# Matmul operands at equal SBUF places, and a gate stage without GpSimd's share, in a two-layer hybrid trunk

## The chip, the cores and the metric

The kernel runs on one core of a Trainium2 chip. The metric is the device time of one execution in microseconds; lower is better. The program is one long, fully unrolled list of instructions for five engines: TensorE (PE in the profile; PEld are its weight loads), VectorE (DVE), ScalarE (ACT), GpSimd (POOL) and SyncE (SP), which here only issues DMAs.

## The reference, cut to what matters

Two layers act on 1024 positions of 1024 features. Layer 0 mixes positions with multi-head latent attention, layer 1 with gated linear attention (GLA). Each is followed by a gated convolutional FFN, and every residual sum goes through a LayerNorm. At the end of each layer an embedding is added through a gate:

```python
for i in range(DEPTH):                     # DEPTH = 2
    m = mla_mixer(x, ...) if i % 2 == 0 else gla_mixer(x, ...)
    x = layer_norm(DN_ALPHA * x + m, ln1_g[i], ln1_b[i])
    x = layer_norm(DN_ALPHA * x + conv_ffn(x, ...), ln2_g[i], ln2_b[i])
    gate = jax.nn.sigmoid(x @ ple_w_gate[i] + ple_b_gate[i])
    x = x + gate * (p[i] @ ple_w_proj[i])
```

The last two lines are the gate stage of this text.

## The kernel before, in words

**Split matmuls.** The results must have nearly float32 precision. Each operand is therefore kept as two float32r tiles, a high part `hi` and a residual `lo`; `mm3` (L178) makes a product of three matmuls: lo times hi, hi times lo, hi times hi. Weights are loaded as float32 by a DMA and split by `split`: ScalarE writes the high part, GpSimd or VectorE the low part (L139, L141).

**Layouts.** The residual stream is `acc`, eight tiles of 128 positions by 1024 features. Matmuls need it feature-major, so TensorE transposes blocks of it (with `ident`), and the result `xt` is two halves `f` of 512 positions, each with a high and a low tile of 8 blocks `k`.

**Order.** Instructions stand in the order in which a planner put them when the program was built, from dependences and its own cost model; each engine then works through its list in order. `tc.issue_after(ins)` keeps an instruction behind another one on its engine. Tiles come from pools; a buffer that is reused is waited for.

**Places.** A pool's tiles lie one behind the other in each partition of the SBUF. `pos_i`, eight int32 of 32 bytes, lies in the pool `mla`, and all pools opened behind it on the same side start 32 bytes further on. `pos_f` (32 bytes) and `blk` (120 bytes) shift what follows them in the same way. In the compiled program the places modulo 256 bytes are: query products `cq` 0 and `wq` 224; the first stage `win` 0 and `xT` 160; scores `kk`, `q`, `r` 0 and `ckv` 224; values `pT`, `vv` 0; output product `wo` and `o` 224; and down, up, gate and GLA products 224 for both operands.

**The gate stage.** The second LayerNorm of a layer is done by halves in `layer_norm_half`. `normalize` makes mean and deviation per tile and writes the normalised tile back to `acc`, without gain and bias. `turned` (L672, L666) transposes four blocks of 128 into a PSUM block of 512 and ScalarE writes it, with gain and bias, to `y`. VectorE copies `y` to the high part (L683), and GpSimd (every first block) or VectorE (every second) subtracts to get the low part (L684). Half 0 is done while the down projection of the FFN (`dn_ps`, additions at L1058) still runs on the tiles of half 1; half 1 is done in `ple`, under the first gate matmuls.

`ple` runs over two column halves `c` and eight tiles `t`: 24 matmuls for the gate (`g_ps`), 6 for the projected embedding (`pr_ps`). VectorE adds the gate's bias (L1142), ScalarE takes the sigmoid (L1143), VectorE multiplies with the projection (L1144) and adds the product to `acc` (L1145). As `acc` lacks gain and bias, `residual` applies them once per tile when `c` is 0: GpSimd multiplies with the gain's row (L815), VectorE adds the bias's row (L817), 1024 elements each. `turn_p` transposes the embeddings into `pT` (L1104 to L1106).

In layer 0 `feature_major` (L1117 to L1120) turns each finished tile for the GLA. It writes to new tiles `nx` in the buffers of `xt`, so it starts when the gate matmuls of half 0 are done: tiles 0 to 3 are turned behind the gate tiles 4 to 7, tiles 4 to 7 behind the last one. The GLA then starts with its gates (`a_ps` L1255, L1259).

Of the kernel before, what the change touches and what calls it, by code (L numbers as in the profile page):

```python
# [7 lines left out]
F32 = mybir.dt.float32  # L8
F32R = mybir.dt.float32r
BF16 = mybir.dt.bfloat16  # L10
I32 = mybir.dt.int32
AF = mybir.ActivationFunctionType
ALU = mybir.AluOpType
# [3 lines left out]
P = 128  # L17
S = 1024
D = 1024
NT = S // P  # L20
HALF = 512
# [21 lines left out]
def hybrid_trunk_kernel(ctx: ExitStack, tc: tile.TileContext, a: dict, out: bass.AP):  # L43
    nc = tc.nc
# [33 lines left out]
    neg_half = cpool.tile([P, 4], F32, name="neg_half")  # L78
    nc.vector.memset(neg_half, -0.5)
    half_pi = cpool.tile([P, 1], F32, name="half_pi")  # L80
    nc.vector.memset(half_pi, HALF_PI)

    par = {}
# [124 lines left out]
    with tc.tile_pool(name="pa", bufs=1) as pa, tc.tile_pool(name="pa2", bufs=2) as pa2:  # L208
# [21 lines left out]
                split(st, w_in[k][0][:, c0:c1], w_in[k][1][:, c0:c1], nc.vector if k % 2 else nc.gpsimd)  # L230


        pos_i = mla.tile([P, NT], I32, name="pos_i")
        nc.sync.dma_start(pos_i, a["positions"][0].rearrange("(t p) -> p t", p=P))
        pos_f = pa.tile([P, NT], F32, name="pos_f")
        nc.vector.tensor_copy(pos_f, pos_i)
        inv_b = pa.tile([P, 32], F32, name="inv_b")
        nc.sync.dma_start(inv_b, a["c_inv"].partition_broadcast(P))
# [383 lines left out]
            for f in range(2)  # L622
        ]

    ln_end = [None, None]
    fm_end = [None]

    xs = [dram.tile([P, D], F32, name=f"xs_{t}") for t in range(NT)]
# [26 lines left out]
    def turned(f, i, which, k, y, wide=True):  # L655

        g, b = par[f"ln{which}g", i], par[f"ln{which}b", i]
        if wide:
            y2 = big(f"y_ps_{i}_{which}_{f}_{k}")
            yps = [y2[:, :512], y2[:, 512:]]  # L660
        else:
            yps = [one(f"y_ps_{i}_{which}_{f}_{k + n}") for n in range(2)]
        for n in range(2):
            kn = k + n
            turn_block(f, kn, yps[n])
            nc.scalar.activation(  # L666
                y[:, n * HALF : (n + 1) * HALF], yps[n], AF.Identity, bias=b[:, kn : kn + 1], scale=g[:, kn : kn + 1]
            )

    def turn_block(f, k, dst):  # L670
        for tt in range(4):
# [2 lines left out]
    def layer_norm_half(f, i, which, tmp, xt, wide=True):  # L674

        normalize(f, i, which)
        for k in range(0, 8, 2):
            y = tmp.tile([P, S], F32, tag="tmp", name=f"y_{i}_{which}_{f}_{k}")
            turned(f, i, which, k, y, wide)
            for n in range(2):  # L680
                yn = y[:, n * HALF : (n + 1) * HALF]
                hi, lo = xt[f][0][:, k + n, :], xt[f][1][:, k + n, :]
                nc.vector.tensor_copy(hi, yn)  # L683
                ln_end[n] = (nc.vector if n else nc.gpsimd).tensor_tensor(lo, yn, hi, op=ALU.subtract).ins  # L684

    def first_half(i, tmp, xt, ys):

# [114 lines left out]
    def load_rows(pool, i, which):  # L802
# [4 lines left out]
            nc.sync.dma_start(t, a[f"ln{which}_{n}"][i].partition_broadcast(P))  # L807
            rows.append(t)
        return rows

    def residual(ts, rows, after=None):

        for t in ts:
            with tc.issue_after(ln_end[0]):
                nc.gpsimd.tensor_tensor(acc[t], acc[t], rows[0], op=ALU.mult)  # L815
            with tc.issue_after(after or ln_end[1]):
                nc.vector.tensor_tensor(acc[t], acc[t], rows[1], op=ALU.add)  # L817

    def up_stage(i, xt, tmp, sp, xb):

# [265 lines left out]
    def ple(i, xt, tmp, apool, sgp, gb, last):  # L1086
# [22 lines left out]
            turn_p(f)  # L1109
        bg = gb.tile([P, D], F32, tag="rowp", name=f"row_p_{i}")  # L1110
        nc.sync.dma_start(bg, a["ple_b_gate"][i].partition_broadcast(P))
        nx = []

        def feature_major(t):
            yp = big(f"x3_ps_{i}_{t}").rearrange("p (k n) -> p k n", k=8)
            for k in range(8):
                nc.tensor.transpose(yp[:, k, :], acc[t][:, k * P : (k + 1) * P], ident)  # L1117
            hi, lo = (n[:, :, (t % 4) * P : (t % 4 + 1) * P] for n in nx[t // 4])
            fm_end[0] = nc.scalar.copy(hi, yp).ins
            nc.vector.tensor_tensor(lo, yp, hi, op=ALU.subtract)  # L1120

        for c in range(2):
# [8 lines left out]
            for t in range(NT):  # L1131
                tl = slice((t % 4) * P, (t % 4 + 1) * P)
                gp = one(f"g_ps_{i}_{c}_{t}")
                for k in range(8):
                    mm3(gp, both(xt[t // 4], slice(None), k, tl), both(wgs[k // 2], slice(None), k % 2), k == 0, k == 7)
                rp = one(f"pr_ps_{i}_{c}_{t}")
                for k in range(2):
                    mm3(rp, both(pT[k], slice(None), slice(t * P, (t + 1) * P)), both(wpr, slice(None), k), k == 0, k == 1)
                if c == 0:
                    residual((t,), rows2[0])  # L1140
                sg = sgp.tile([P, HALF], F32, tag="sg", name=f"sg_{i}_{c}_{t}")
                nc.vector.tensor_tensor(sg, gp, bg[:, cs], op=ALU.add)  # L1142
                nc.scalar.activation(sg, sg, AF.Sigmoid)  # L1143
                nc.vector.tensor_tensor(sg, rp, sg, op=ALU.mult)  # L1144
                nc.vector.tensor_tensor(acc[t][:, cs], acc[t][:, cs], sg, op=ALU.add)  # L1145
                if last:
                    nc.sync.dma_start(out[0, t * P : (t + 1) * P, cs], acc[t][:, cs])
                elif c and t >= 4:
                    if not nx:
                        nx.extend(new_xt(f"x3_{i}"))  # L1150
                    feature_major(t - 4)
        if not last:
            for t in range(4, NT):
                feature_major(t)
        return nx

    def open_up(i, xt, tmp):

# [51 lines left out]
    with ExitStack() as pg:  # L1210
# [17 lines left out]
        def gates(g0):  # L1228
# [11 lines left out]
            tri = g0.tile([P, P], F32R, name="tri")  # L1240
            nc.vector.tensor_copy(tri, st[:, :P])

            blk = g0.tile([P, 30], F32R, name="blk")
            nc.vector.tensor_copy(blk, st[:, P : P + 30])
            w2 = g0.tile([2 * RANK + 1, 512], F32, name="w2")
            for r in range(2):
# [276 lines left out]
```

## Time and profile before

| | us |
|---|---|
| median of 3 runs | 3052.33 (3052.01 to 3053.41) |
| the profiled execution | 3054.3 |
| its span, first to last instruction | 3052.5 |
| PE busy | 2922.6 (96%) |
| DVE busy | 1725.6 (57%) |
| POOL busy | 1339.9 (44%) |
| ACT busy | 1251.5 (41%) |

The busy times are those of one profiled execution. Matmuls overlap in the pipeline, so their busy time is longer than their pace; the pace is read from starts or from the length of unbroken pieces. The mean granted clock of TensorE is 0.984 of 2.4 GHz; the profile knows two levels, 2.4 and 1.2 GHz.

### The profile page before, as it was taken

How to read it: one execution, taken by the hardware profiler on the slowest of the kernel's cores; microseconds unless marked ns; L12 is line 12 of the kernel's file. 1: busy time of each engine (PE TensorE's matmuls, PEld its weight loads, DVE VectorE, ACT ScalarE, POOL GpSimd, SP SyncE). 2: the span in 40 equal slices, each digit the busy share in tenths (PEclk: the TensorE clock that was granted, in tenths of full speed). 3: DMA queues.
4: the chain of work that ended last, by engine and by line, in shares of the span. 5: the costliest groups of instructions: out<-in, count | busy, mean ns of one | idle time of the engine just before them, and what ended most of it. 6: DMA issues, size and time to landing. Idle time of an engine off the chain costs nothing.

```text
span 3052.5 us, 36344 instructions
## 1 busy us (share of the span) xinstructions
PE 2922.6 (96%) x13938; PEld 2407.8 (79%) x13938; DVE 1725.6 (57%) x2815; ACT 1251.5 (41%) x2022; POOL 1339.9 (44%) x904
## 2 busy tenths in 40 slices
PE   8999999999988999999998999999979999999979
PEld 7878888888866888878877678888758888778867
DVE  5546666666675555545577444544765555545693
ACT  3325555555555444441131243333554544512231
POOL 4331101010056777765744113223358777666560
PEclk9999999999999999999999999999989999999999
DMA  3464212121123222253311102112122222343211
GB/s 117 134 236 155 70 54 67 56 68 52 37 83 97 83 83 82 78 171 97 124 49 37 48 23 63 30 47 62 62 83 85 82 83 76 118 138 118 90 49 49
DMA packets 197784, 254.66 MB, mean 83 GB/s; under 512 B 11297, under 2 KB 133961, under 8 KB 195562
## 3 DMA queue, kind: packets, MB, share of 16 engines
q1 hardware_dynamic: 193354, 230.32, 23.8%
q10 hardware_dynamic: 4256, 22.02, 2.0%
q8 instruction: 109, 1.79, 0.2%
q14 instruction: 65, 0.53, 0.1%
HBM read 191.49 MB, written 60.82 MB: 83 GB/s over the span
## 4 chain that ended last, share of the span: by engine, by line
PE 76%; DVE 7%; ACT 5%; POOL 4%; issue 4%; DMA 1%; SPq 0%; POOLq 0%; ACTq 0%; DVEq 0%
PE up_u L178 13%; PE dn_ps L178 13%; PE up_g L178 11%; PE g_ps L178 4%; PE m_ps L178 4%; PE gkv_ps L178 4%; PE o_ps L178 3%; PE gr_ps L178 3%; PE q_ps L178 3%; PE gm_ps L178 2%; PE pT_ps L542 2%; PE qr_ps L178 1%; PE k_ps L178 1%; PE v_ps L178 1%; ACT pr L526 1%
## 5 line engine op out<-in xcount | busy, mean ns | idle before, releaser
L178 PE MATMUL up_u<-xT_hi,wT 128*128 128x512 f32 x1056 | 346.4, 394 | 20.6 <-ACT acc L914 15.5
L1058 DVE TENSOR_TENSOR acc<-dn_ps,acc 128x512 f32<-128x512 f32 x320 | 220.0, 689 | 168.1 <-PE dn_ps L178 167.4
L178 PE MATMUL dn_ps<-wdn_hi,a_lo 128*128 128x512 f32 x704 | 277.0, 393 | 9.9 <-ACT acc L1054 6.4
L178 PE MATMUL dn_ps<-wdn_hi,a_hi 128*128 128x512 f32 x704 | 275.8, 392 | 0.0
L178 PE MATMUL dn_ps<-wdn_lo,a_hi 128*128 128x512 f32 x704 | 275.6, 391 | 0.0
L178 PEld LDWEIGHTS up_u<-xT_hi,wT 128*128 128x128 f32 x1056 | 200.2, 190 | 71.4 <-issue 19.2
L178 PE MATMUL up_g<-x_hi,wB 128*128 128x512 f32 x704 | 235.1, 394 | 5.2 <-DVE mv L639 1.6
L141 POOL TENSOR_TENSOR wo_lo<-wo_st,wo_hi 128x1024 fp32r<-128x1024 f32 x16 | 38.5, 2407 | 453.9 <-ACT wo_hi L139 453.9
L141 POOL TENSOR_TENSOR wT<-ws_S,wT 128x512 fp32r<-128x512 f32 x128 | 165.7, 1295 | 120.1 <-ACT wT L139 119.4
L178 PE MATMUL up_u<-xT_lo,wT 128*128 128x512 f32 x528 | 207.8, 394 | 0.0
L178 PE MATMUL m_ps<-wo_hi,o 128*128 128x512 f32 x512 | 190.8, 415 | 0.0
L141 POOL TENSOR_TENSOR wdn_lo<-wdn_st,wdn_hi 128x1024 fp32r<-128x1024 f32 x44 | 106.0, 2415 | 166.5 <-ACT wdn_hi L139 145.1
L139 ACT CAST wdn_hi<-wdn_st 128x1024 fp32r<-128x1024 f32 x44 | 45.7, 1048 | 304.9 <-PE dn_ps L178 287.2
L178 PEld LDWEIGHTS dn_ps<-wdn_hi,a_lo 128*128 128x128 f32 x704 | 133.0, 189 | 40.6 <-ACT acc L1054 8.1
L178 PEld LDWEIGHTS up_g<-x_hi,wB 128*128 128x128 f32 x704 | 132.0, 188 | 40.7 <-ACT acc L911 7.0
L178 PEld LDWEIGHTS dn_ps<-wdn_hi,a_hi 128*128 128x128 f32 x704 | 132.8, 189 | 27.8
L178 PEld LDWEIGHTS dn_ps<-wdn_lo,a_hi 128*128 128x128 f32 x704 | 133.1, 189 | 26.8
L141 POOL TENSOR_TENSOR wB<-wup_g,wB 128x512 fp32r<-128x512 f32 x84 | 111.3, 1329 | 85.4 <-ACT wB L139 85.3
L923 DVE TENSOR_TENSOR up_g<-up_g,acc 128x512 f32<-128x512 f32 x44 | 30.8, 700 | 208.2 <-PE up_g L178 201.3
L544 ACT CAST pT<-pT_ps 128x512 fp32r<-128x512 f32 x192 | 89.3, 475 | 139.2 <-PE pT_ps L542 136.9
L178 PE MATMUL o_ps<-pT,vv 128*128 128x512 f32 (+3 forms) x576 | 142.5, 350 | 3.8 <-ACT pT L544 2.9
L178 PE MATMUL up_g<-x_lo,wB 128*128 128x512 f32 x352 | 137.4, 390 | 0.2 <-DVE x_lo L702 0.2
(363 smaller groups left out, 8155.9 us busy)
## 6 DMA issues: line engine op xcount, KB each, us to landing
a_s<-acc SPq DMA_DIRECT2D x44, 512.0 KB
a_st<-a_s SPq DMA_DIRECT2D x44, 512.0 KB
wdn_st<-in_ffn_w_down_dram SPq DMA_DIRECT2D x44, 512.0 KB
wup_g<-in_ffn_w_up_dram SPq DMA_DIRECT2D x42, 512.0 KB
wup_u<-in_ffn_w_up_dram SPq DMA_DIRECT2D x42, 512.0 KB
q<-q_s SPq DMA_DIRECT2D x32, 512.0 KB
q_s<-qo ACTq DMA_DIRECT2D x14, 1024.0 KB
r<-r_s SPq DMA_DIRECT2D x32, 256.0 KB
```

Source lines behind the costliest of these rows:

```text
L139: nc.scalar.copy(hi, src)
L141: lo_last[0] = (lo_eng or nc.gpsimd).tensor_tensor(lo, src, hi, op=ALU.subtract).ins
L178: nc.tensor.matmul(ps, w[a_], x[b_], start=start and n == 0, stop=stop and n == 2, skip_group_check=more)
L526: nc.scalar.activation(pr, pr, AF.Copy, scale=ri)
L542: nc.tensor.transpose(tp[:, i * P : (i + 1) * P], prs[i][:, kb * P : (kb + 1) * P], ident)
L544: nc.scalar.copy(pT[:, 0, off:], tp[:, off:])
L923: nc.vector.tensor_tensor(g1, g1, self.u2, op=ALU.add)
L1058: put[t, c] = nc.vector.tensor_tensor(y, dp, y, op=ALU.add).ins
```

## The change

- `pos_i` moves to the first pool, padded to 64 int32; `pos_f` is padded to 32 elements, `blk` to 64. Both operands of all matmuls of the products get equal places modulo 256 bytes.
- In `layer_norm_half` ScalarE writes the high part itself from the PSUM block, a second time with gain and bias, in place of VectorE's copy of `y`. All low parts are VectorE's.
- `residual` is gone. Per half tile, behind the product with the projection, VectorE multiplies the half of `acc` with the gain's row, adds the bias's row to the gated product, and adds the two.
- `feature_major` writes into `xt` itself, in the columns of a tile whose gate matmuls are done, and so follows every gate tile of `c` = 1 by one; only tile 7 is left behind the last.

```diff
+    pos_i = cpool.tile([P, 64], I32, name="pos_i")[:, :NT]
...
-        pos_i = mla.tile([P, NT], I32, name="pos_i")
         nc.sync.dma_start(pos_i, a["positions"][0].rearrange("(t p) -> p t", p=P))
-        pos_f = pa.tile([P, NT], F32, name="pos_f")
+        pos_f = pa.tile([P, 32], F32, name="pos_f")[:, :NT]
...
+        return yps
...
-            turned(f, i, which, k, y, wide)
+            yps = turned(f, i, which, k, y, wide)
             for n in range(2):
-                yn = y[:, n * HALF : (n + 1) * HALF]
-                hi, lo = xt[f][0][:, k + n, :], xt[f][1][:, k + n, :]
-                nc.vector.tensor_copy(hi, yn)
-                ln_end[n] = (nc.vector if n else nc.gpsimd).tensor_tensor(lo, yn, hi, op=ALU.subtract).ins
+                kn, yn = k + n, y[:, n * HALF : (n + 1) * HALF]
+                hi, lo = xt[f][0][:, kn, :], xt[f][1][:, kn, :]
+                nc.scalar.activation(
+                    hi, yps[n], AF.Identity, bias=par[f"ln{which}b", i][:, kn : kn + 1], scale=par[f"ln{which}g", i][:, kn : kn + 1]
+                )
+                nc.vector.tensor_tensor(lo, yn, hi, op=ALU.subtract)
...
-    def residual(ts, rows, after=None):
-
-        for t in ts:
-            with tc.issue_after(ln_end[0]):
-                nc.gpsimd.tensor_tensor(acc[t], acc[t], rows[0], op=ALU.mult)
-            with tc.issue_after(after or ln_end[1]):
-                nc.vector.tensor_tensor(acc[t], acc[t], rows[1], op=ALU.add)
...
-            hi, lo = (n[:, :, (t % 4) * P : (t % 4 + 1) * P] for n in nx[t // 4])
+            hi, lo = (n[:, :, (t % 4) * P : (t % 4 + 1) * P] for n in xt[t // 4])
...
-                if c == 0:
-                    residual((t,), rows2[0])
                 sg = sgp.tile([P, HALF], F32, tag="sg", name=f"sg_{i}_{c}_{t}")
                 nc.vector.tensor_tensor(sg, gp, bg[:, cs], op=ALU.add)
                 nc.scalar.activation(sg, sg, AF.Sigmoid)
-                nc.vector.tensor_tensor(sg, rp, sg, op=ALU.mult)
-                nc.vector.tensor_tensor(acc[t][:, cs], acc[t][:, cs], sg, op=ALU.add)
+                sgi = nc.vector.tensor_tensor(sg, rp, sg, op=ALU.mult).ins
+                y = acc[t][:, cs]
+                with tc.issue_after(sgi):
+
+                    nc.vector.tensor_tensor(y, y, rows2[0][0][:, cs], op=ALU.mult)
+                    nc.vector.tensor_tensor(sg, sg, rows2[0][1][:, cs], op=ALU.add)
+                    nc.vector.tensor_tensor(y, y, sg, op=ALU.add)
                 if last:
                     nc.sync.dma_start(out[0, t * P : (t + 1) * P, cs], acc[t][:, cs])
-                elif c and t >= 4:
-                    if not nx:
-                        nx.extend(new_xt(f"x3_{i}"))
-                    feature_major(t - 4)
+                elif c and t:
+                    feature_major(t - 1)
         if not last:
-            for t in range(4, NT):
-                feature_major(t)
-        return nx
+            feature_major(NT - 1)
+        return xt
...
-            blk = g0.tile([P, 30], F32R, name="blk")
+            blk = g0.tile([P, 64], F32R, name="blk")[:, :30]
```

## Rows read from the trace of the kernel before

**Rows 1.** The page: share of the chain that ended last, by engine.
```profile
PE 76%; DVE 7%; ACT 5%; POOL 4%; issue 4%; DMA 1%; SPq 0%; POOLq 0%; ACTq 0%; DVEq 0%
```

**Rows 2.** Windows: length, busy times of PE, PEld, DVE, ACT, POOL, clock, DMA share, GB/s.
```profile
1580.00:1640.00 60.00, 44.26 (x186) 34.28 (x184) 51.88 (x52) 17.70 (x22) 41.72 (x24) 0.86 0.13 36
2908.00:2966.00 58.00, 42.02 (x193) 32.67 (x194) 52.88 (x53) 18.31 (x23) 43.12 (x24) 0.94 0.13 41
1724.70:1781.50 56.80, 49.54 (x195) 30.76 (x193) 38.77 (x57) 29.70 (x42) 12.84 (x5) 0.88 0.26 75
```

**Rows 3.** The chain in order of time: start, length, engine, tile, line, count.
```profile
124.78 11.20 PE q_ps L178 x48
...
425.42 1.39 PE m_ps L178 x6
...
1358.19 193.47 PE dn_ps L178 x852
...
1654.14 5.44 PE g_ps L178 x24
```

**Rows 4.** Timeline of PE, first stage: start, length, instruction; 17 starts apart.
```profile
79.81 0.40 PE L178 MATMUL h_ps<-win_hi,xT_lo 128*128 128x512 f32 x1
...
83.78 0.40 PE L178 MATMUL h_ps<-win_hi,xT_hi 128*128 128x512 f32 x1
```

**Rows 5.** Timeline of PE in the GLA, behind transposes; eight starts apart each.
```profile
1871.76 0.40 PE L178 MATMUL gr_ps<-x_hi,gwr_hi 128*128 128x512 f32 x1
...
1873.62 0.39 PE L178 MATMUL gr_ps<-x_lo,gwr_hi 128*128 128x512 f32 x1
...
1875.43 0.39 PE L178 MATMUL gr_ps<-x_hi,gwr_lo 128*128 128x512 f32 x1
```

**Rows 6.** Groups of DVE from 1560 to 1646: busy us, mean ns, idle before.
```profile
L817 DVE TENSOR_TENSOR acc<-acc,row_b 128x1024 f32<-128x1024 f32 x8 | 18.8, 2353 | 0.0
L684 DVE TENSOR_TENSOR x_lo<-y,x_hi 128x512 fp32r<-128x512 f32 x8 | 14.6, 1831 | 0.1
```

**Rows 7.** Timeline of DVE and POOL from 1603 to 1646.
```profile
1603.03 0.41 DVE L683 CAST x_hi<-y 128x512 fp32r<-128x512 f32 x1
...
1609.03 23.34 POOL L815 TENSOR_TENSOR acc<-acc,row_g 128x1024 f32<-128x1024 f32 x8
...
1617.33 3.35 DVE L817 TENSOR_TENSOR acc<-acc,row_b 128x1024 f32<-128x1024 f32 x1
...
1640.12 1.21 DVE L817 TENSOR_TENSOR acc<-acc,row_b 128x1024 f32<-128x1024 f32 x1
```

**Rows 8.** Groups of ACT from 1560 to 1646.
```profile
L666 ACT ACTIVATE y<-y_ps,par 128x512 f32<-128x512 f32 x16 | 11.7, 776 | 5.8 <-PE y_ps L672 5.6
```

**Rows 9.** Waits from 1575 to 1650: total us, times, longest.
```profile
PE pT_ps L1104 <- DVE pT_lo L1106: 8.0, 1, 8.0
...
PE pr_ps L178 <- POOL wpr_lo L141: 2.9, 1, 2.9
...
PE dn_ps L178 <- DVE acc L1058: 1.6, 1, 1.6
```

**Rows 10.** Timeline of PE from the last gate matmul to the GLA's gates.
```profile
1724.69 1.91 PE L1117 MATMUL x_ps<-ident,acc 128*128 128x128 f32 x16
1730.35 3.33 PE L1117 MATMUL x_ps<-ident,acc 128*128 128x128 f32 x16 [3.75 <-DVE x_lo L1120]
...
1744.53 3.59 PE L1255 MATMUL a_ps<-x_hi,aw 128*32 128x512 f32 x8 [1.05 <-DVE ge L1267]
```

**Rows 11.** Groups of DVE from 1646 to 1724, GpSimd mostly idle.
```profile
L1145 DVE TENSOR_TENSOR acc<-acc,sg 128x512 f32<-128x512 f32 x12 | 8.3, 693 | 0.4
...
L1142 DVE TENSOR_TENSOR sg<-g_ps,row_p 128x512 f32<-128x512 f32 x12 | 8.3, 691 | 36.0 <-PE g_ps L178 36.0
```

**Rows 12.** Timeline from 1622: ACT writes half 1, PE reads half 0.
```profile
1622.50 0.59 ACT L1105 CAST pT_hi<-pT_ps 128x512 fp32r<-128x512 f32 x1 [11.95 <-PE pT_ps L1104]
...
1622.68 0.63 PE L178 MATMUL pr_ps<-wpr_hi,pT_hi 128*128 128x512 f32 x1
```

More of the change, by code (lines that the diff above doesn't have):

```diff
@@ L623, in new_xt @@
         ]
-    ln_end = [None, None]
     fm_end = [None]
@@ L1111, in ple @@
         nc.sync.dma_start(bg, a["ple_b_gate"][i].partition_broadcast(P))
-        nx = []
         def feature_major(t):
```

## The prediction

> **What bounds the kernel now.** I began with the page, at the chain that ended last: TensorE carries 76% of it, VectorE 7%, ScalarE 5%, GpSimd 4% [rows 1]. So time can come from two places: from the pace of single matmuls, and from the few stretches where TensorE waits. I looked for both.
>
> *Pace.* In the chain, long unbroken pieces of matmuls with 512 columns show it as length over count. The down projection runs 852 in 193.47 us, 227.1 ns each; the query projection runs 48 in 11.20 us, 233.3 ns each; in the attention six matmuls of the output projection take 1.39 us, 231.7 ns each [rows 3]. In the first stage 17 steps from one start to another take 3.97 us, 233.5 ns each [rows 4]. The granted clock is full there, so this is no clock. The places differ: the compiled program of the kernel before puts, modulo 256 bytes, weights and activations of the down projection both at 224, those of the query projection at 224 and 0, those of the first stage at 0 and 160. A stream at equal places is not always fast either: after transposes the GLA projection starts at 232.5 ns a step (8 steps in 1.86 us) and then settles at 226 (8 steps in 1.81 us) [rows 5]. I read this as a pace that has to lock: a long stream at equal places locks after some eight matmuls, a stream at unequal places never does.
>
> *Waits.* The windows show where TensorE loses most. In layer 0 it is busy 44.26 us of the 60 us around the start of the gate stage, at a mean clock of 0.86; in layer 1 42.02 of 58 at 0.94; in the passage from the gate stage to the GLA 49.54 of 56.8 at 0.88 [rows 2]. A mean of 0.86 over the two levels 2.4 and 1.2 GHz means 28% of the stretch at the lower, so the loss is 15.7 us of idling and about 16.8 x 0.74 / 2 = 6.2 us of slow work: 22 us. In the same way layer 1 loses 16.0 + 2.5 = 18.5 us, the passage 7.3 + 5.9 = 13 us.
>
> What TensorE waited for in layer 0 is VectorE above all: 8.0 us for the transposed embeddings' low part, 2.9 us for GpSimd's low part of the projection's weights, 1.6 us for the down projection's additions [rows 9]. VectorE is late because its own instructions are stretched. The residual's addition takes 3.35 us while GpSimd runs its eight multiplications, a block of 23.34 us, and 1.21 us once GpSimd has finished [rows 7]; the mean low part takes 1831 ns and the mean addition 2353 ns [rows 6], against 0.69 us for half the size beside an idle GpSimd [rows 11]. The two engines get in each other's way.
>
> **The change part by part.**
>
> *Places.* Query and rotary products: 384 + 192 = 576 matmuls, 233.3 - 227.1 = 6.2 ns each, 3.6 us. First stage: 192 matmuls of 512 columns, 6.4 ns each, 1.2 us, less the first eight of every run of 24: 0.8 us. Attention: 128 groups of six output matmuls lose 6 x (231.7 - 227.1) = 28 ns each, 3.5 us, and scores and values perhaps as much again. These streams are short and cut by transposes, and the output matmuls were at equal places already, so most of the loss should stay: I take 2.5 us between 0 and 7. The gates' few matmuls get nothing. Sum 7 us, bounds 0 (places do nothing) and 12 (all of it locks).
>
> The Trainium skill (TensorE: Matmul & The Clock Gate, Step-by-step: what each phase is for) speaks against it: matmul data and weights come through two independent read ports, and loading weights takes nothing from the running matmul. By that rule this part is 0; it is a rival below, since rows 3 and 4 show streams that differ in pace.
>
> *High parts on ScalarE.* Each of the 8 blocks of a half loses VectorE's copy and gains a second reading of the same PSUM block, 776 ns [rows 8]. Per half 8 x 0.78 = 6.2 us more on ScalarE. The second half of the norm lies under four gate tiles of the first half. One has 24 matmuls in 5.44 us [rows 3] and six more at the same pace, 6.8 us, so the cover is 27 us. ScalarE works 17.7 us in the 60 us of this window [rows 2]; even if all of it fell under the cover, 24 of 27 us would be full. The first half lies under the last matmuls of the down projection. Without cover the move would cost 6.2 us a half, 25 us in all. The low parts all go to VectorE: four more per half, at about 0.69 us, against eight copies of some 0.41 us saved [rows 7]: nothing on balance.
>
> *GpSimd out of the stage.* Its 8 low parts and 8 multiplications go, and with them the stretching. VectorE's low parts and additions in rows 6 should fall from 14.6 + 18.8 us to about 11 us of low parts, no block of additions. Then the waits of 8.0 and 1.6 us end, and most of the half clock that follows them (I take 4.5 of 6.2 us), with some 1.5 us of shorter ones: about 15.5 us in layer 0. The 2.9 us for the projection's weights stay, as ScalarE's part of that now queues behind more work, and so do the 2 to 3 us until the second half's norm is there. In layer 1 the loss is 18.5 instead of 22 us; with the same 6 to 7 us left I take 12 to 14, say 13.5.
>
> *Residual per half tile.* Before, per tile, one addition of 1024 on VectorE. Now two more instructions of 512 in each of the 16 half tiles. With all inputs in SBUF such an addition takes 693 ns beside an idle GpSimd [rows 11]. VectorE's load is 5 x 0.69 = 3.5 us in each half tile of 6.8 us: hidden; in the passage it has 36 us of idling in 78 us. It shows where nothing follows: at the end of the kernel, 2 x 0.7 us, -1.4 us, and as much at the end of layer 0, which is in the next term.
>
> *Feature-major per tile, in place.* Before, four of the eight tiles were turned behind the last gate matmul, with a wait of 3.75 us for a PSUM buffer, and the second half's product of the GLA gates began at 1744.53 us, 19.8 us after the first of these transposes [rows 10]. Now one is left there; three go into the loop, at 1.91 / 2 = 0.95 us of TensorE each. The last tile needs 4 x 0.7 us of VectorE, 0.95 us of transposes, a copy of 1024 on ScalarE (at most 2 x 776 ns) and a low part of 1024 on VectorE (1.2 us), some 6.5 us, mostly under the first half's gate products. The GLA's start has its own chain of weights and exponentials, so I take 5 us of the 13, between 0 and 9.
>
> *Sum.* 7 + 15.5 + 13.5 + 5 - 1.4 = 40 us, off 3054.3 us of the profiled execution (span 3052.5): 3014 us. That execution lay 2.0 us above the median of the runs, so 3012 us.
>
> **Rivals.**
>
> *A. Places do nothing* (the rule above; or the slow streams have another cause, as the equally placed output matmuls hint). Then 33 us: 3019. Chance 0.14. For it: equal places were slow in attention. Against: 576 matmuls that never settle, in unbroken streams of 48.
>
> *B. ScalarE becomes the new wait.* Its queue is in order; a PSUM pair of the transposes is held by four readings instead of two, 1.55 us longer, and sigmoids and weight casts stand behind them. If 0.75 us per block is exposed in half of the four halves and the clock drops again, 12 + 4 us come back: 3028. For it: 776 ns against about 0.4 us on VectorE. Against: ScalarE waited for VectorE or TensorE most of that time. Chance 0.16.
>
> *C. Slower: the in-place writing waits by whole tile.* The turned tile is written into columns of the very tile that the next gate matmuls read. If readers and writers waited for the tile and not for its columns, each of seven tiles would stop TensorE for the two copies, 1.5 + 1.2 us, 19 us in all, and at half clock the seven tiles of 6.8 us would take up to 48 us more. The 40 us won are gone once the clock is halved for 44% of that (19 + 21 us); at three quarters the kernel is 15 us slower, 3067. Against it: the embeddings' second half was written from 1622.50 us while a matmul read the first half of that tile from 1622.68 us [rows 12]. Chance 0.04.
>
> *D. The stage does not get faster*, since VectorE is late for another reason: 3046 to 3053, chance 0.04. The 3.35 against 1.21 us speaks against it.
>
> **How the numbers follow.** My case, with the sum as above, has 0.62; its own range is 3001 to 3022 (passage 0 to 9, places 0 to 12, fronts 22 to 35). A and B reach 3030; C and D, with half of B's tail, stay outside. The range is 2997 to 3031. A run of this kernel agrees within about 0.05%, and 0.2% (6 us) is what can be told from no change. Faster by more than that are my case, A, B and a little of D: 0.93; the same: 0.03; slower: 0.04.
>
> **What would show it.** Right: query matmuls at 227 ns; no GpSimd work in the gate stage but weights and the norm's small steps; low parts at 0.6 to 0.7 us; TensorE without a wait of 8 us at the start of the gate stage, clock at least 0.95 there; one set of transposes behind the last gate matmul. Wrong: query matmuls still at 233 ns (A); TensorE waiting for ScalarE's high parts or PSUM (B); a gap before each gate tile of the second column half (C); the largest uncertainty is how much of the two fronts' 40 us is really given back.

## The result, and the profile after

The changed kernel takes 3008.98 us (median of 4 runs, 3006.64 to 3011.36), the kernel before beside it 3052.87; the ratio is 0.985, 95% interval 0.9834 to 0.9867: about 44 us faster. The forecast was 3012, in a range from 2997 to 3031. The profiled execution took 3010.44 us, its span is 3008.7. Of the later executions of the changed kernel one took 14282 us; it stands in none of the ranges below. The sum behind the forecast fits less well than its end: the term for the two gate stages is 12.6 us too small, those for places and passage are too large, and 4.7 us were lost in stretches that gain nothing by the change or too little to be seen.

The page's chain by engine, against [rows 1]: TensorE's share has grown from 76 to 79%.

```profile
PE 79%; DVE 6%; ACT 5%; POOL 3%; issue 3%; DMA 1%; SPq 0%; POOLq 0%; ACTq 0%; DVEq 0%
```

Windows of the lengths of [rows 2], laid to the same matmuls (columns as there):

```profile
1575.75:1635.75 60.00, 58.86 (x283) 47.61 (x282) 38.18 (x69) 30.21 (x41) 12.43 (x12) 1.00 0.15 44
2878.80:2936.80 58.00, 56.89 (x274) 45.96 (x273) 37.87 (x68) 30.62 (x42) 12.42 (x12) 1.00 0.21 69
1704.64:1761.44 56.80, 49.87 (x192) 32.06 (x191) 36.46 (x56) 27.46 (x40) 10.87 (x5) 0.91 0.26 75
```

At the start of both gate stages TensorE now works 58.86 of 60 and 56.89 of 58 us, at full clock; before it was 44.26 and 42.02 us at 0.86 and 0.94. The third row, the passage to the GLA, is nearly what it was.

The chain's pieces that answer to [rows 3], and two starts in the first stage, 17 steps apart, as in [rows 4]:

```profile
126.15 10.88 PE q_ps L180 x48
...
428.69 1.39 PE m_ps L180 x6
...
1359.95 191.16 PE dn_ps L180 x842
```

```profile
81.69 0.39 PE L180 MATMUL h_ps<-win_hi,xT_lo 128*128 128x512 f32 x1
...
85.55 0.39 PE L180 MATMUL h_ps<-win_hi,xT_hi 128*128 128x512 f32 x1
```

The query product runs at 10.88 / 48 = 226.7 ns a matmul where it took 233.3, the first stage at 3.86 / 17 = 227.1 where it took 233.5. Six output matmuls of the attention take the same 1.39 us.

Groups of DVE and ACT from 1560 to 1646, for [rows 6, 8], and TensorE's only wait from 1575 to 1650, for [rows 9]:

```profile
L666 ACT ACTIVATE y<-y_ps,par 128x512 f32<-128x512 f32 x16 | 12.5, 795 | 0.5 <-PE y_ps L673 0.4
...
L687 DVE TENSOR_TENSOR x_lo<-y,x_hi 128x512 fp32r<-128x512 f32 x16 | 12.0, 782 | 1.5 <-ACT x_hi L684 1.5
L684 ACT ACTIVATE x_hi<-y_ps,par 128x512 fp32r<-128x512 f32 x16 | 11.7, 801 | 0.0
```

```profile
PE y_ps L673 <- ACT acc L650: 1.1, 1, 1.1
```

VectorE's low parts take 782 instead of 1831 ns, and the waits of 8.0, 2.9 and 1.6 us are all gone. Before, VectorE also had the copies in this window, a group that [rows 6] leaves out:

```profile
L683 DVE CAST x_hi<-y 128x512 fp32r<-128x512 f32 x16 | 12.3, 790 | 4.0 <-ACT y L666 4.0
```

Set against each other by stretches, from one matmul that both kernels have to the next (lengths worked out from the two traces):

| stretch, in us | before | after | |
|---|---|---|---|
| start to the first query product | 98.6 | 100.2 | +1.6 |
| query and rotary products | 137.4 | 132.8 | -4.6 |
| attention, first norm | 643.8 | 643.1 | -0.7 |
| up and down products, layer 0 | 682.9 | 686.0 | +3.1 |
| second norm and first column half, layer 0 | 105.3 | 83.1 | -22.2 |
| second column half, passage, to the GLA's first output product | 178.4 | 176.0 | -2.4 |
| GLA, up and down products, layer 1 | 1044.6 | 1044.3 | -0.3 |
| second norm and first column half, layer 1 | 102.5 | 83.1 | -19.4 |
| second column half, layer 1 | 54.4 | 54.2 | -0.2 |
| last matmul to the end | 4.6 | 5.9 | +1.3 |

The column adds up to -43.8, the difference of the spans. Below, "the front" is the second norm with the first column half, and "the passage" the row from the second column half on.

The end of the kernel (timeline of DVE): four instructions behind the last projection where two stood.

```profile
3002.93 0.69 DVE L1137 TENSOR_TENSOR sg<-pr_ps,sg 128x512 f32<-128x512 f32 x1 [0.74 <-ACT sg L1136]
3003.54 0.68 DVE L1141 TENSOR_TENSOR acc<-acc,row_g 128x512 f32<-128x512 f32 x1
3004.14 0.68 DVE L1142 TENSOR_TENSOR sg<-sg,row_b 128x512 f32<-128x512 f32 x1
3004.86 0.69 DVE L1143 TENSOR_TENSOR acc<-acc,sg 128x512 f32<-128x512 f32 x1
```

The passage (timeline from 1703 to 1711), to be set beside [rows 10]:

```profile
1703.18 7.78 SPq L165 DMA_DIRECT2D gwr_st<-in_gla_w_in_dram  x2
...
1704.64 1.47 PE L1111 MATMUL x_ps<-ident,acc 128*128 128x128 f32 x12
...
1707.10 1.04 ACT L141 CAST gwr_hi<-gwr_st 128x1024 fp32r<-128x1024 f32 x1 [2.26 <-DMA gwr_st<-in_gla_w_in_dram]
1708.05 1.01 ACT L1114 CAST x_hi<-x_ps 128x1024 fp32r<-128x1024 f32 x1
...
1709.09 1.22 DVE L1115 TENSOR_TENSOR x_lo<-x_ps,x_hi 128x1024 fp32r<-128x1024 f32 x1 [2.29 <-ACT x_hi L1114]
...
1710.45 0.77 PE L180 MATMUL gq_ps<-x_hi,gwq_lo 128*128 128x512 f32 x1 [4.34 <-DVE x_lo L1115]
```

Twelve transposes stand behind the last projection before the wait and four behind it: two tiles of eight, 6 and 7. Tile 6 is turned by about 1705.6, but ScalarE copies it at 1708.05 only: its queue is in order, and a cast of weights that stands ahead waits 2.26 us for its DMA. The next product needs the PSUM buffer and waits 4.34 us. Before, the transposes themselves waited 3.75 us for such a buffer.

### The profile page after: what moved, and what is told of

Same layout as the page of the kernel before. It is cut to its first block, busy times and chain, and to the rows that moved or that the text cites. A ratio compares the mean times of both kernels' runs of the same rounds, so it can differ in the third digit from the quotient of the medians.

```text
span 3008.7 us, 36380 instructions
## 1 busy us (share of the span) xinstructions
PE 2906.1 (97%) x13938; PEld 2401.6 (80%) x13938; DVE 1688.3 (56%) x2847; ACT 1272.6 (42%) x2054; POOL 1266.8 (42%) x872
## 4 chain that ended last, share of the span: by engine, by line
PE 79%; DVE 6%; ACT 5%; POOL 3%; issue 3%; DMA 1%; SPq 0%; POOLq 0%; ACTq 0%; DVEq 0%
PE dn_ps L180 14%; PE up_u L180 14%; PE up_g L180 11%; PE g_ps L180 5%; PE m_ps L180 4%; PE gkv_ps L180 4%; PE o_ps L180 3%; PE gr_ps L180 3%; PE q_ps L180 3%; PE gm_ps L180 2%; PE pT_ps L543 2%; PE qr_ps L180 1%; PE pr_ps L180 1%; PE k_ps L180 1%; ACT pr L527 1%
```

## The experiments

Each time is compared with runs of the kernel before on the same chip. Where a few us matter, the stretches of the trace decide, since runs of one kernel differ by 5 to 15 us.

### Places alone

```diff
+    pos_i = cpool.tile([P, 64], I32, name="pos_i")[:, :NT]
...
-        pos_i = mla.tile([P, NT], I32, name="pos_i")
...
-        pos_f = pa.tile([P, NT], F32, name="pos_f")
+        pos_f = pa.tile([P, 32], F32, name="pos_f")[:, :NT]
...
-            blk = g0.tile([P, 30], F32R, name="blk")
+            blk = g0.tile([P, 64], F32R, name="blk")[:, :30]
```

> The kernel before with the three shifts of places alone; the gate stage stays as it was. Theory (equal places decide the pace): query and rotary products go from 233.3 to about 227 ns a matmul (576 of them, 3.6 us), the first stage's 192 products of 512 columns from 7.1 to about 1.5 ns above the settled pace (1 us), attention hardly moves (under 1 us), the gate stage keeps its waits of 8 us in layer 0 and 7 us in layer 1: about 3048 us. Rival (the faster query pace came from something else that the new kernel does): query matmuls stay at 233 ns and the time stays at 3053.

Measured: 3046.7 us, ratio 0.9981 (0.9971 to 0.999). A piece of the chain and the longest waits of TensorE from 1575 to 1660:

```profile
127.10 10.88 PE q_ps L179 x48
```

```profile
PE pT_ps L1104 <- DVE pT_lo L1106: 6.5, 1, 6.5
PE pr_ps L179 <- POOL wpr_lo L142: 2.9, 1, 2.9
```

The query product has its 226.7 ns, and the gate stage its waits; the fronts take 102.5 and 104.1 us, where the kernel before took 105.3 and 102.5: so much do two traces of an unchanged front differ. Places gain about 6 us in the whole (3 to 9 by the interval) and nothing that shows in the gate stage.

### Query operands 64 bytes apart, first stage 128

```diff
+    qpool.tile([P, 16], F32, name="pad_q")
     cq = tuple(qpool.tile([P, 4, S], F32R, name=f"cq_{n}") for n in ("hi", "lo"))
...
-        pos_f = pa.tile([P, 32], F32, name="pos_f")[:, :NT]
+        pos_f = pa.tile([P, 64], F32, name="pos_f")[:, :NT]
```

> The changed kernel with the query activations moved by 64 bytes against their weights, and the first stage's weights by 128 bytes against its activations; all else at equal places. Theory (places must be equal modulo 256): both streams are slow again, 233.3 and 233.5 ns a matmul, 3.6 + 0.8 = 4.4 us, 3013 us. Rival 1 (a period of 64 bytes is enough): both stay at about 227 ns, 3009. Rival 2 (a period of 128): the query stream is slow and the first stage stays fast, 3012.5.

Measured: 3008.19 us, ratio 0.9856 (0.9842 to 0.9871), which by itself tells nothing at this size. The chain's pieces do:

```profile
126.92 10.99 PE q_ps L180 x48
...
198.18 11.20 PE q_ps L180 x48
```

229.0 ns a matmul early and 233.3 later; the first stage, 128 bytes apart, takes 232 to 233.5 ns over 17 steps. A period of 64 bytes is refuted.

### The distances exchanged: query 128 bytes, first stage 64

```diff
+    qpool.tile([P, 32], F32, name="pad_q")
     cq = tuple(qpool.tile([P, 4, S], F32R, name=f"cq_{n}") for n in ("hi", "lo"))
...
-        pos_f = pa.tile([P, 32], F32, name="pos_f")[:, :NT]
+        pos_f = pa.tile([P, 48], F32, name="pos_f")[:, :NT]
```

> The two distances of the run with 64 and 128 bytes exchanged: query activations 128 bytes from their weights modulo 256, the first stage's operands 64 bytes apart. Theory (only equal places modulo 256 lock): both streams stay slow most of the time, the query matmuls 4 to 7 ns and the first stage's 4 to 7 ns above the settled pace. Rival (128 bytes apart is as good as equal for a long stream, and the first stage was slow there since its runs are short): the query matmuls at under 1 ns above it, 227 ns.

Measured: 3013.2 us (one run). A piece of the chain:

```profile
125.88 11.15 PE q_ps L180 x48
```

That is 232.3 ns, and the first stage takes 233.5 over 17 steps. Neither 64 nor 128 bytes apart does what equal places do.

### Most weights moved by 32 bytes

```diff
     acc = [accp.tile([P, D], F32, name=f"acc_{t}") for t in range(NT)]
+    accp.tile([P, 8], F32, name="pad_w")
...
-            blk = g0.tile([P, 64], F32R, name="blk")[:, :30]
+            blk = g0.tile([P, 56], F32R, name="blk")[:, :30]
```

> The changed kernel with most of the weights, and the small weights of attention, moved by 32 bytes, at 192 instead of 224 modulo 256, while activations stay at 224; the attention's output product has both at 192. Theory (equality decides): the long streams of 512 columns (576 query, 1428 + 1908 up, 1920 down, 672 gate, 192 + 384 + 384 GLA products, 7464 in all) lose about 6.2 ns each, 46 us, less the first matmuls of each run: 3045 to 3055; the output product of attention, equal at 192, keeps its pace. Rival 1 (a place of its own is bad, not the difference: activations at 0 were): no change, 3009. Rival 2 (the query stream was special): only the query part, 3.6 us, 3012.5.

Measured: 3041.59 us, ratio 0.9965 (0.9952 to 0.9978), 33 us slower than the changed kernel. Pieces of the chain: the down product, the attention's output product (both operands at 192), and the GLA's product with 384 columns:

```profile
412.56 1.39 PE m_ps L180 x6
...
1369.93 203.01 PE dn_ps L180 x870
...
1791.26 8.33 PE gkv_ps L180 x48
```

The down product goes from 191.16 / 842 = 227.0 to 203.01 / 870 = 233.3 ns, so the query stream was not special: the same activations, still at 224, get slow when their weights move to 192. Whether 224 is special is open. Six output matmuls at 192 and 192 take what they took at 224 and 224, but groups so short don't reach the fast pace at 224 either, and every long stream that ran fast in any run had both operands at 224. The third row has the same length as in the changed kernel (8.35 us for 48), though its operands now lie 32 bytes apart: at 384 columns the places did nothing. Both rivals, as they were written, are refuted. The loss is smaller than 46 us: by pace the 3336 up matmuls would lose 3336 x 6.2 = 20.7 us, yet against two traces of the changed kernel the up stretches grew by 6.3 to 7.8 and 4.0 to 6.9 us. The waits of 0.5 us and more stay as they were there, but starts held up briefly, 0.26 to 0.5 us apart, fall from 186 and 166 in the two traces to 106. So part of the slower pace is taken back from such delays; why is open.

### VectorE's copies back

```diff
-                nc.scalar.activation(
-                    hi, yps[n], AF.Identity, bias=par[f"ln{which}b", i][:, kn : kn + 1], scale=par[f"ln{which}g", i][:, kn : kn + 1]
-                )
+                nc.vector.tensor_copy(hi, yn)
```

> The changed kernel with VectorE's copy for the high parts as before; the low parts and the residual stay as changed, so GpSimd stays out of the stage. Theory (GpSimd's absence is what made the stage fast): VectorE has 8 copies of about 0.41 us more per half, 3.3 us, mostly under the gate matmuls: 3009 to 3013, no wait of TensorE over 3 us at the start of the gate stages. Rival (ScalarE's high parts are what removed the waits): waits of 5 us or more come back in both layers and the clock falls: 3018 to 3030.

Measured: 3023.28 us, ratio 0.9903 (0.9888 to 0.9918). The fronts take 90.0 us each, 6.9 more than in the changed kernel. TensorE's longest wait from 1575 to 1657, and VectorE beside GpSimd:

```profile
PE pT_ps L1097 <- DVE pT_lo L1099: 4.4, 1, 4.4
```

```profile
1597.32 2.95 DVE L684 CAST x_hi<-y 128x512 fp32r<-128x512 f32 x2
...
1597.56 2.43 POOL L143 TENSOR_TENSOR wpr_lo<-wpr_st,wpr_hi 128x1024 fp32r<-128x1024 f32 x1 [3.19 <-ACT wpr_hi L141]
...
1600.02 2.51 POOL L143 TENSOR_TENSOR wg_lo<-wg_st,wg_hi 128x1024 fp32r<-128x1024 f32 x1
...
1600.19 3.49 DVE L685 TENSOR_TENSOR x_lo<-y,x_hi 128x512 fp32r<-128x512 f32 x2
...
1603.60 0.42 DVE L684 CAST x_hi<-y 128x512 fp32r<-128x512 f32 x1
```

The theory as it was written is refuted, and the rival's time came true, though its longest wait stayed just under 5 us: ScalarE's high parts matter. A copy takes 0.42 us alone, but two take 2.95 us and two low parts 3.49 while GpSimd splits weights, which it still does in the changed kernel. From 1560 to 1657 the copies take:

```profile
L684 DVE CAST x_hi<-y 128x512 fp32r<-128x512 f32 x16 | 9.8, 630 | 0.2 <-ACT y L666 0.2
```

Of these 9.8 us, 16 x 0.42 = 6.7 us is the copies' own time and 3.1 us the stretching. Which of the two makes the 6.9 us of the front isn't separated: no run has the copies on VectorE and GpSimd wholly idle.

### The residual as before, with GpSimd

```diff
+            nc.gpsimd.tensor_tensor(acc[t], acc[t], rows[0], op=ALU.mult)
+            with tc.issue_after(ln_end[1]):
+                nc.vector.tensor_tensor(acc[t], acc[t], rows[1], op=ALU.add)
...
-                    nc.vector.tensor_tensor(y, y, rows2[0][0][:, cs], op=ALU.mult)
-                    nc.vector.tensor_tensor(sg, sg, rows2[0][1][:, cs], op=ALU.add)
-                    nc.vector.tensor_tensor(y, y, sg, op=ALU.add)
+                nc.vector.tensor_tensor(acc[t][:, cs], acc[t][:, cs], sg, op=ALU.add)
```

> The changed kernel with the residual as before: eight multiplications of 1024 on GpSimd and eight additions of 1024 on VectorE in the first column half of each gate stage; high parts stay on ScalarE, low parts on VectorE. Theory (GpSimd's block stretches VectorE): low parts and additions of VectorE go from some 0.7 and 1.2 us to 1.8 to 3 us under the block, TensorE waits several us for the embeddings' low parts again and its clock falls: 5 to 12 us a layer, 3019 to 3033 us. Rival (the copies and low parts of the norm were what delayed VectorE; the residual is hidden): 3009, no wait over 2 us in the first column half.

Measured: 3025.59 us, ratio 0.9904 (0.9888 to 0.9919). The fronts take 93.2 and 93.7 us, 10.0 and 10.6 us more. TensorE's longest wait from 1575 to 1657, and the timeline of DVE and POOL:

```profile
PE y_ps L674 <- ACT acc L651: 4.5, 1, 4.5
```

```profile
1583.97 7.49 POOL L819 TENSOR_TENSOR acc<-acc,row_g 128x1024 f32<-128x1024 f32 x3
1591.42 0.54 POOL L644 TENSOR_TENSOR rs<-ve,neg_half 128x1 f32<-128x1 f32 x1
...
1612.46 11.51 POOL L819 TENSOR_TENSOR acc<-acc,row_g 128x1024 f32<-128x1024 f32 x4 [0.84 <-PE y_ps L674]
...
1613.30 0.67 DVE L1110 TENSOR_TENSOR pT_lo<-pT_ps,pT_hi 128x512 fp32r<-128x512 f32 x1
...
1614.26 4.13 DVE L688 TENSOR_TENSOR x_lo<-y,x_hi 128x512 fp32r<-128x512 f32 x2 [0.29 <-ACT x_hi L685]
...
1618.31 0.68 DVE L1110 TENSOR_TENSOR pT_lo<-pT_ps,pT_hi 128x512 fp32r<-128x512 f32 x1
...
1618.91 6.14 DVE L821 TENSOR_TENSOR acc<-acc,row_b 128x1024 f32<-128x1024 f32 x2
```

Under the block of 11.51 us VectorE's instructions with both inputs in SBUF take 2 to 3 us each, while L1110, which reads one input from PSUM, keeps its 0.67. So it is not VectorE as such that is slowed. The Trainium skill (SBUF — State Buffer, Who interferes with whom) says the same: an instruction of VectorE with two SBUF inputs contends with a GpSimd instruction that reads SBUF; one with at most one SBUF input, outside the modes that use both ports, does not. The trace agrees for these two kinds, 2.07 us beside 0.67. The copies of the run above, with one SBUF input, were stretched as well, so they are no case of that exception; their mode isn't shown by any run. A second way shows in the first two rows: the norm's small steps (L644) stand behind three multiplications in GpSimd's queue, and TensorE waits 4.5 us for the normalised tile. That order is this run's own; in the kernel before, the multiplications were held behind the norm. The wait that the expectation named, for the embeddings' low parts, did not come back. So the time came out as forecast, but in part by another way, and the 10.0 us are not the price of the stretching alone.

### The full-size residual, all on VectorE

```diff
-            nc.gpsimd.tensor_tensor(acc[t], acc[t], rows[0], op=ALU.mult)
+            with tc.issue_after(ln_end[0]):
+                nc.vector.tensor_tensor(acc[t], acc[t], rows[0], op=ALU.mult)
```

(against the run above)

> The same full-size residual per tile, but with both steps on VectorE and nothing on GpSimd. Theory (it is the two engines in each other's way): 16 instructions of about 1.2 us in each first column half, some 2.4 + 2.1 us of VectorE in each tile of 6.8 us, hidden; low parts keep their 0.7 us: 3007 to 3012 us. Rival (it is the order: full-size steps that stand ahead of the embeddings' low parts on VectorE): waits of TensorE of 5 us or more at the second half of the embeddings in both layers, 3019 to 3030.

Measured: 3007.51 us, ratio 0.9843 (0.9828 to 0.9858). Groups of DVE from 1560 to 1657:

```profile
L688 DVE TENSOR_TENSOR x_lo<-y,x_hi 128x512 fp32r<-128x512 f32 x16 | 12.3, 786 | 3.2 <-ACT x_hi L685 3.2
L819 DVE TENSOR_TENSOR acc<-acc,row_g 128x1024 f32<-128x1024 f32 x8 | 9.7, 1216 | 0.0
L821 DVE TENSOR_TENSOR acc<-acc,row_b 128x1024 f32<-128x1024 f32 x8 | 9.7, 1215 | 0.0
```

The fronts take 83.1 us each, as in the changed kernel. Full-size steps on VectorE, and none of them seen: the gain is in taking the residual off GpSimd; doing it per half tile adds nothing. As this run also puts the multiplications behind the norm again (`issue_after`), it doesn't tell how much of the 10.0 us was the stretching and how much the order; a run with GpSimd's multiplications behind the norm is missing.

### Every first low part back on GpSimd

```diff
-                nc.vector.tensor_tensor(lo, yn, hi, op=ALU.subtract)
+                (nc.vector if n else nc.gpsimd).tensor_tensor(lo, yn, hi, op=ALU.subtract)
```

> The changed kernel with every first low part of the norm back on GpSimd; high parts stay on ScalarE, the residual on VectorE. Of the 22.2 us that the stretch from the first transposes of the norm to the second column half lost in layer 0, putting VectorE's copies back returned 6.9 us, and GpSimd's multiplications 10.0. Theory (the three shares add up): the low parts return the rest, about 5 us a layer: 3015 to 3021 us. Rival (the low parts cost nothing alone, and the rest comes only when several work together): 3007 to 3011.

Measured: 3012.58 us, ratio 0.9868 (0.9853 to 0.9883). The fronts take 84.7 us, 1.6 more in each layer. Groups of DVE from 1560 to 1657, and TensorE's waits:

```profile
L1143 DVE TENSOR_TENSOR acc<-acc,sg 128x512 f32<-128x512 f32 x9 | 8.4, 935 | 0.2
L687 DVE TENSOR_TENSOR x_lo<-y,x_hi 128x512 fp32r<-128x512 f32 x8 | 8.3, 1042 | 2.4 <-ACT x_hi L684 2.3
...
L1137 DVE TENSOR_TENSOR sg<-pr_ps,sg 128x512 f32<-128x512 f32 x10 | 6.9, 690 | 8.1 <-ACT sg L1136 8.1
```

```profile
PE pr_ps L180 <- POOL wpr_lo L143: 1.0, 1, 1.0
```

The same pattern (935 and 1042 ns with SBUF inputs, 690 with one from PSUM), and part of the wait for the projection's weights is back. Theory and rival both miss: alone the low parts cost 1.6 us. Put back one by one, the parts return 6.9 + 10.0 + 1.6 = 18.5 of layer 0's 22.2 us and 6.9 + 10.6 + 1.6 = 19.1 of layer 1's 19.4. In the run with places alone layer 0's front was 2.8 us shorter than in the first trace, which leaves 0.9, so no share that needs several at work together is shown.

### The GLA's operand turned as before

```diff
-            hi, lo = (n[:, :, (t % 4) * P : (t % 4 + 1) * P] for n in xt[t // 4])
+            hi, lo = (n[:, :, (t % 4) * P : (t % 4 + 1) * P] for n in nx[t // 4])
...
-                elif c and t:
-                    feature_major(t - 1)
+                elif c and t >= 4:
+                    if not nx:
+                        nx.extend(new_xt(f"x3_{i}"))
+                    feature_major(t - 4)
         if not last:
-            feature_major(NT - 1)
-        return xt
+            for t in range(4, NT):
+                feature_major(t)
+        return nx
```

> The changed kernel with the GLA's operand turned as before: in new tiles, four tiles behind the last gate matmul. Theory (the passage gained nothing, since another wait took the place of the old one): from the first gate matmul of the second column half to the first product of the gate r the kernel takes as long as the changed one, within 3 us: 3007 to 3013 us. Rival (the prediction's term of 5 us was right and is hidden in the sum by something else): 5 us longer there, 3014.

Measured: 3007.45 us, ratio 0.9847 (0.9823 to 0.987). TensorE's longest wait from 1690 to 1790:

```profile
PE x_ps L1113 <- DVE x_lo L1117: 3.7, 1, 3.7
```

The passage takes 175.9 us, against 176.0 and, in a second trace of the changed kernel below, 178.1: the old wait is back, and no loss by it is seen. A term of 5 us hidden by something else would have shown; it is not there.

### Weights of the gate r behind the turned copy, and a shorter end

```diff
-                w = wload(kxn(w_in, 0, 8, 2048 + h * GDV + j * P, P), 8, P, f"gwr_{h}_{j}", after=(fm_end[0] if h == 0 and j else None, None))
+                w = wload(kxn(w_in, 0, 8, 2048 + h * GDV + j * P, P), 8, P, f"gwr_{h}_{j}", after=(fm_end[0] if h == 0 else None, None))
...
+                y = acc[t][:, cs]
+                end = last and c and t == NT - 1
+                if end:
+                    nc.vector.tensor_tensor(y, y, rows2[0][0][:, cs], op=ALU.mult)
+                    nc.vector.tensor_tensor(y, y, rows2[0][1][:, cs], op=ALU.add)
...
```

> The changed kernel with two edits: the split of the first weights of the gate r stands behind the last turned copy on ScalarE's queue, and in the last half tile of the kernel gain and bias are applied before the projection's product. Theory (in the passage ScalarE stands waiting for the DMA of those weights while the turned tile 6 is ready, and TensorE waits for that tile 4.3 us and then works at half clock): the wait and 2 to 3 us of half clock go, 5 to 7 us; the end becomes 1.3 us shorter: 3001 to 3003 us. Rival (the weights are late then, and the first product of r waits as long): the passage stays, only the end gains, 3008.

Measured: 3005.81 us, ratio 0.9845 (0.9825 to 0.9866). TensorE's waits in the passage:

```profile
PE rev_ps L1280 <- ACT E L1282: 2.5, 1, 2.5
PE gq_ps L180 <- DVE x_lo L1115: 2.0, 1, 2.0
```

The wait of 4.34 us falls to 2.0, so ScalarE's stop at the DMA was about half of it. But the next wait, in the GLA's gates, grows from 1.9 to 2.5 us, and the passage takes 175.0 us: 1 to 3 us less than the two traces of the changed kernel, of the 5 to 7 expected, and no more than they differ by. From the last matmul to the end it is 4.6 us, 1.3 less, as expected.

### The same, and the last tile of layer 0 too

```diff
-                end = last and c and t == NT - 1
+                end = c and t == NT - 1
```

(against the run above)

> The changed kernel with the weights of the gate r split behind the last turned copy, and with gain and bias applied before the projection's product in the last half tile of both layers. Theory: the kernel's end is 1.3 us shorter; in layer 0 the last tile's chain is 1.3 us shorter too, and TensorE's wait for a PSUM buffer there, 4.3 us in the changed kernel and 2.0 us with the weights' split moved alone, falls to about 1 us: 2 to 4 us faster than the changed kernel on the same chip. Rival (the chain of the GLA's gates sets the passage): only the end gains, 1 to 2 us.

Measured: 3006.26 us, ratio 0.9842 (0.9828 to 0.9855). The end, timeline of DVE:

```profile
3003.72 0.69 DVE L1142 TENSOR_TENSOR sg<-pr_ps,sg 128x512 f32<-128x512 f32 x1 [0.74 <-ACT sg L1136]
3004.45 0.69 DVE L1147 TENSOR_TENSOR acc<-acc,sg 128x512 f32<-128x512 f32 x1
```

Two instructions are left at the end, and the passage takes 173.2 us. The wait for the PSUM buffer stays at 2.3 us where about 1 was expected, so the last tile's chain is not what holds it.

### The changed kernel again

> The changed kernel once more, as it is, beside the run that shortens the passage and the end: 3005 to 3011 us. In its trace the stretches that no edit touches (start to the first latents, up and down products) may each differ by 1 to 2 us from the first profile: if so, the 1.9 us that the down products of layer 0 lost and the 1.5 us of layer 1's up products are no work of the change; if they come back the same, they are.

Measured: ratio 0.9837 (0.9824 to 0.9851), 3001.51 to 3008.52 us. The run above does not beat it; its 1.3 us at the end and some 3 us in the passage are below what the times can tell. In the second trace of the changed kernel the way to the first query product takes 98.5 us, layer 0's up and down products 682.8 and the passage 178.1. So +1.6, +3.1 and -2.4 in the table are no more than what two runs of one kernel differ by, and none of them is shown to be the change's work. The fronts do not wander so: 83.1 us in both layers, to 0.1 us, in this trace and in the other runs with the same gate stage and pace.

## Why the prediction was right, and where its sum was not

*The bound.* Right: pace and waits were two sources, and both gave time.

*Places, 7 us.* The mechanism is right, the size is not. Query and rotary products give 576 x 6.6 = 3.8 us, as worked out; their stretch is shorter by 1.5 to 4.6 us in the runs with this same pace, 4.6 in the table being the upper end. The first stage gains 6.4 ns on most of its 192, about 1 us, which its stretch can't show, as two traces of the changed kernel differ by 1.7 us in it. Operands 64 and 128 bytes apart and the shifted weights show that unequal places are slow; that equal ones other than 224 are fast is not shown. The term for attention, 2.5 us, does not show: six output matmuls take 1.39 us before and after, and the stretch, 643.8 us before, lies between 640.2 and 644.8 in the twelve traces with these places. The prediction had the reason in hand, that these streams are short and cut by transposes, and still took a third of the upper bound. By the Trainium skill (TensorE: Matmul & The Clock Gate, Step-by-step: what each phase is for), with two independent read ports for data and weights, the whole term of places would be 0; the 6.6 ns here and the 33 us of the shifted weights differ from that, and the measurement decides. Why equal places lock is open.

*The fronts, 15.5 + 13.5 us.* Measured 22.2 + 19.4. The neighbour was right: VectorE was late, and mainly beside GpSimd. Of the pieces that the prediction priced, the low parts alone are worth 1.6 us a layer and the residual up to 10.0 to 10.6, part of it by the order of that run; a third, the copies, was priced at nothing. The low parts come to 782 ns rather than 600 to 700, since GpSimd still splits weights there. The step that failed is that 2.9 us for the projection's weights and 2 to 3 us for the second half's norm would stay, and part of the half clock. All went: the clock is 1.00 and one wait of 1.1 us is left. With more work queued on ScalarE, the weights are no longer waited for, which the prediction ruled out. The wait is gone with GpSimd's share, and 1.0 us of it is back with the low parts alone.

*High parts on ScalarE, nothing on balance.* Wrong by its price. The exchange of four low parts for eight copies was costed at one copy's 0.41 us, beside an idle GpSimd, while the group of copies in the same trace took 790 ns on average, 12.3 us in the window. Taking them away is worth 6.9 us a layer; the copies' own time and their stretching both go, and their shares are open.

*Residual per half tile.* Hidden as predicted, and 1.3 us at the end against 1.4.

*Feature-major in place, 5 us.* Wrong. Three sets of transposes did move into the loop, but from five to two behind the last gate matmul, not from four to one: tile 3 stood there before, as tile 6 does now. The passage is 2.4 us shorter, within what runs of one kernel differ by, and turning as before shows no cost. The prediction saw the wait for a PSUM buffer and took it to go; it moved from the transposes to the next product. With that wait halved, the passage got shorter by no more than two traces differ by, and a wait in the gates' chain grew by 0.6 us.

*Rivals.* A fell with the pace. B did not happen where it was placed: in the front no wait of TensorE names the high parts. It came in another place, in the passage, with ScalarE's queue standing at a DMA. C fell, as far as the trace goes: in the second column half of layer 0 no wait of TensorE is shown before the last tile. D fell.

*The sum.* 4.6 + 0.7 + 22.2 + 19.4 + 2.4 + 0.5 in the stretches that got shorter, less 1.3 at the end and 4.7 in the way to the first query product and the up and down products of layer 0, is 43.8 us, against 40 forecast. The end agrees better than the terms, and that was luck: 12.6 us too little in the fronts stood against some 4 too much in places and passage, and against 4.7 that two runs differ by anyway.

## What to carry to other kernels

Before an instruction is priced, look at what the neighbour on the other engine does at that moment: under GpSimd's work an instruction of VectorE with its inputs in SBUF cost two to three and a half times its own time here, and one with a PSUM input cost the same. Take the price from the mean of the group, not from one row. Long unbroken streams of fp32r matmuls with 512 columns are worth laying at equal places modulo 256 bytes (tried at 224 only); groups of six between transposes show no gain. Read it from length over count of the chain's pieces, since the whole time doesn't show 3 us. When a wait is removed ahead of a chain of dependent steps, follow the buffer to its next user before counting the gain.

## What was not expected of the hardware

- Matmuls of 512 columns with operands 32, 64, 96 and 128 bytes apart modulo 256 took 233.3, 229.0 to 233.5, 233.5 and 232.0 to 233.5 ns, ones both at 224 226.7 to 227.9; with 384 columns 48 took 8.35 us at equal places and 8.33 at 32 bytes apart.
- A copy of 128x512 from SBUF to SBUF on VectorE took 0.42 us alone, and two took 2.95 us beside GpSimd.
